# GLA's q and k in a stage of their own with seven products for eight, the gate's adaLN dots in quarters inside GLA, and a regrouped start

## The chip, the cores and the metric

The kernel runs on one core of a Trainium2 chip. The metric is the device time of one execution in microseconds. Every number comes from a profiled execution or from timed runs. The engines are called as in the profile: PE (TensorE), DVE (VectorE), ACT (ScalarE), POOL (GpSimd) and SP (SyncE); PEld is PE's loading of weights. SP and POOL also issue DMAs, each on a queue of its own.

## What is computed

A decoder layer with two parallel branches on x of 512 tokens by 2048 channels, all in float32. An adaLN modulation of x is projected; a gated linear attention (GLA, 4 heads, dk 256, dv 512) and a gated delta rule (GDN, 16 heads) run side by side; sigmoid gates merge them; an output projection, the adaLN gate, the residual and a layer norm follow.

```python
ada = jax.nn.silu(c) @ w_ada + b_ada
shift, scale, gate = jnp.split(ada, 3, axis=-1)
h = x * (1 + scale[:, None, :]) + shift[:, None, :]
u = h @ w_in
(gla_q, gla_k, gla_v, gla_g, gla_lr, gdn_q, gdn_k, gdn_v, gdn_z, gdn_b, gdn_a,
 merge_g) = jnp.split(u, _split_offsets(), axis=-1)
log_a = jax.nn.log_sigmoid((gla_lr @ w_gk2 + b_gk2).astype(f32)) / GLA_GATE_NORM
o_gla = _gla_chunked(_heads(gla_q...), _heads(gla_k...), _heads(gla_v...), _heads(log_a...))
y_gla = _gated_rmsnorm(o_gla, gla_norm_w, gla_g).astype(dt)
...
g_a, g_b = jnp.split(jax.nn.sigmoid(merge_g), 2, axis=-1)
merged = g_a * (y_gla @ w_branch[0]) + g_b * (y_gdn @ w_branch[1])
out = merged @ w_out
r = DEEPNORM_ALPHA * x + gate[:, None, :] * out
return _layernorm(r, ln_g, ln_b).astype(dt)
```

## The kernel before

**Products.** Each float32 operand is split into a high part and a low part, and a product is three matmuls, high by high, low by high and high by low (`mm3`, L99). The activation h lies in SBUF as 16 pairs `acth`, `actl` of 128 channels by 512 tokens. A unit of weights is 128x1024: SP loads it (512 KB, `wraw`), ACT rounds it to `whi` (L86), DVE subtracts to `wlo` (L88); `unit()` keeps three of them ahead. A column tile (`col_steps`, `proj_col`, L104 to L114) gives 128 output channels by 512 tokens: two units, 16 channel blocks, 48 matmuls of 512 columns. `proj_row` (L119) gives v in 192 such matmuls.

**The stages, in order of time.** Start: for each of the 16 blocks of h two dots on DVE (`ada_dot`, 128x2048 against silu of c, L215), two small operations into `scs`, then ACT makes `hf` (L247) and `acth` (L94) and DVE `actl` (L96). PE works on eight accumulators at a time and takes the blocks of h in three groups, (0,4), (4,9), (9,16), each for an "early" and a "first" set of columns; between groups the accumulators are drained into `part`, by ACT the first time (L279) and by DVE after (L281). GDN follows, with merge tiles woven in. (A merge tile is a column tile of the merge gates, put through tanh and stored to `d_mg`.) Then GLA, `gla_all`: per head q and k (four column tiles, L739 to L742), the decays `cum` (L743 to L755), the near diagonals (L767 to L799), v by `proj_row` (L801), levels 2 to 6 (L811 to L841, each with an `e` made of cum, k and q by DVE and ACT and sixteen small matmuls), the attention matrix `at` with its parts `atGt`, `atF`, `atqf` (L877 to L896), and four gate tiles (L907 to L915). Then a stage with the adaLN gate's 16 dots of 128x2048 (1 MB each through SP) beside seven merge tiles (L920 to L930). Last the branch products, the output projection and the layer norm; POOL's queue loads their inputs.

**What sets the order.** A scheduler writes each engine's instructions into one fixed row, from the program's text and its buffers; every engine takes its row in order, and an instruction that waits holds up all behind it. So where an instruction stands in the row matters as much as where it stands in the code.

## Time and profile before

| | us |
|---|---|
| median of 3 runs (lowest to highest) | 2410.5 (2410.38 to 2410.74) |
| the profiled execution | 2410.16 |
| its span, first to last instruction | 2408.4 |
| PE busy in the span | 2367.4 (98%) |
| DVE, ACT, POOL busy | 1510.7 (63%), 1054.5 (44%), 80.3 (3%) |
| granted TensorE clock, mean | 0.998 |

The profiled execution is 0.34 us below the median, and 1.8 us of it lie outside the span. A window row gives, for a stretch of the span, each engine's busy time with the number of its instructions. A row of the list of PE's waits says what PE stood for, in total, how often and at the longest. A timeline row is one instruction: its start, its length and, in square brackets, the idle time of the engine just before it with what ended it. The records of matmuls overlap, since they are pipelined: what one costs is read from the distance of starts, not from its length.

### The profile page before, as it was taken

The page shows a single profiled execution, that of the slowest core. Times are in us where ns is not written, and L with a number is a line of the kernel's source. Part 1 is how long each engine was busy: PE and PEld are TensorE (multiplying, and loading weights), DVE is VectorE, ACT ScalarE, POOL GpSimd, SP SyncE. Part 2 cuts the span into 40 slices and gives each one's busy share as a digit, 9 for nine tenths or more (in the row PEclk, how much of TensorE's full clock was granted, in tenths as well). Part 3 has the DMA queues.
Part 4 walks back from the last instruction along what each step waited for, and adds up shares of the span by engine and source line. Part 5 has one row for each costly group of instructions (what it writes and reads, how often), then busy time and mean ns, then how long its engine had stood idle before and what let it go on. Part 6 is the DMA issues. An engine that isn't in the chain of part 4 may idle for free.

```text
span 2408.4 us, 30754 instructions
## 1 busy us (share of the span) xinstructions
PE 2367.4 (98%) x11788; PEld 1943.4 (81%) x11788; DVE 1510.7 (63%) x2787; ACT 1054.5 (44%) x1647; POOL 80.3 (3%) x159
## 2 busy tenths in 40 slices
PE   6999999999999999999999999999999999999997
PEld 5888787888888888878888888888887888888886
DVE  7865677888777788873562745627475322344676
ACT  4335455555665555553442544425424311222353
POOL 0000000000000000000000000000002101010010
PEclk9999999999999999999999999999999999999999
DMA  9964333333333333233223222232298644445674
GB/s 393 369 216 136 114 100 100 100 100 102 100 100 103 108 104 96 96 96 119 94 75 110 88 91 88 76 114 88 92 350 284 214 140 138 146 147 184 215 246 148
DMA packets 119763, 347.92 MB, mean 144 GB/s; under 512 B 32448, under 2 KB 34880, under 8 KB 113472
## 3 DMA queue, kind: packets, MB, share of 16 engines
q1 hardware_dynamic: 109696, 313.45, 38.4%
q0 software_dynamic: 9920, 32.51, 3.9%
q8 instruction: 92, 1.51, 0.3%
q14 instruction: 55, 0.45, 0.1%
HBM read 318.57 MB, written 27.34 MB: 144 GB/s over the span
## 4 chain that ended last, share of the span: by engine, by line
PE 90%; DVE 4%; DMA 3%; issue 1%; ACT 1%; SPq 0%; POOL 0%; POOLq 0%; ACTq 0%; DVEq 0%
PE pj L100 22%; PE pj L101 21%; PE pj L102 21%; PE ms L158 2%; PE ms L157 2%; PE ms L159 2%; PE pj L133 2%; PE pj L134 2%; PE pj L135 2%; PE ms L100 1%; PE ms L102 1%; PE ms L101 1%; PE ms L840 1%; DVE junk L215 1%; DVE wlo L88 1%
## 5 line engine op out<-in xcount | busy, mean ns | idle before, releaser
L100 PE MATMUL pj<-acth,whi 128*128 128x512 f32 x2160 | 870.2, 403 | 20.8 <-ACT acth L94 19.2
L101 PE MATMUL pj<-acth,wlo 128*128 128x512 f32 x2160 | 845.2, 391 | 2.7 <-DVE wlo L88 2.7
L102 PE MATMUL pj<-actl,whi 128*128 128x512 f32 x2160 | 842.8, 391 | 0.0
L88 DVE TENSOR_TENSOR wlo<-wraw,whi 128x1024 fp32r<-128x1024 f32 x414 | 505.1, 1221 | 430.7 <-ACT whi L86 422.6
L86 ACT CAST whi<-wraw 128x1024 fp32r<-128x1024 f32 x414 | 433.7, 1048 | 585.4 <-PE pj L102 383.6
L100 PEld LDWEIGHTS pj<-acth,whi 128*128 128x128 f32 x2160 | 406.7, 188 | 101.4 <-ACT acth L94 20.0
L102 PEld LDWEIGHTS pj<-actl,whi 128*128 128x128 f32 x2160 | 405.9, 188 | 87.4 <-DVE actl L96 0.4
L101 PEld LDWEIGHTS pj<-acth,wlo 128*128 128x128 f32 x2160 | 407.0, 188 | 78.2 <-DVE wlo L88 4.1
L667 DVE TENSOR_TENSOR tmp<-vi,mi 128x8 f32<-128x8 f32 (+30 forms) x496 | 145.9, 294 | 13.3
L671 DVE TENSOR_REDUCE vi<-tmp 128x4 f32<-128x8 f32 (+30 forms) x496 | 111.1, 224 | 13.1
L215 DVE SCALAR_TENSOR_TENSOR junk<-wada,cs 128x2048 f32<-128x2048 f32 x48 | 109.7, 2285 | 4.7 <-DMA wada<-in_wada_dram 4.3
L100 PE MATMUL pj<-yh,whi 128*128 128x512 f32 x256 | 100.9, 394 | 0.0
L101 PE MATMUL pj<-yh,wlo 128*128 128x512 f32 x256 | 100.9, 394 | 0.0
L102 PE MATMUL pj<-yl,whi 128*128 128x512 f32 x256 | 100.9, 394 | 0.0
L158 PE MATMUL ms<-wlo,yh 128*128 128x512 f32 x240 | 94.8, 395 | 0.5 <-DVE wlo L88 0.5
L157 PE MATMUL ms<-whi,yh 128*128 128x512 f32 x240 | 93.8, 392 | 0.0
L159 PE MATMUL ms<-whi,yl 128*128 128x512 f32 x240 | 93.2, 388 | 0.0
L399 DVE SCALAR_TENSOR_TENSOR ac<-upad,convw,ac 128x512 f32<-128x512 f32 x96 | 71.5, 744 | 11.2 <-ACT ac L397 9.6
L133 PE MATMUL pj<-whi,acth 128*128 128x512 f32 x192 | 74.9, 390 | 0.0
L134 PE MATMUL pj<-wlo,acth 128*128 128x512 f32 x192 | 74.9, 390 | 0.0
L135 PE MATMUL pj<-whi,actl 128*128 128x512 f32 x192 | 74.7, 389 | 0.0
L100 PEld LDWEIGHTS pj<-yh,whi 128*128 128x128 f32 x256 | 47.9, 187 | 12.0
(304 smaller groups left out, 2768.8 us busy)
## 6 DMA issues: line engine op xcount, KB each, us to landing
wada<-in_wada_dram SPq DMA_DIRECT2D x48, 1024.0 KB, 8.7
wraw<-in_wqkv_dram SPq DMA_DIRECT2D x90, 512.0 KB, 3.4
wraw<-in_wbr_dram SPq DMA_DIRECT2D x64, 512.0 KB, 3.9
wraw<-in_wout_dram SPq DMA_DIRECT2D x64, 512.0 KB, 4.3
wraw<-in_wmg_dram SPq DMA_DIRECT2D x40, 512.0 KB, 3.6
wraw<-in_wz_dram SPq DMA_DIRECT2D x32, 512.0 KB, 3.5
wraw<-in_wlv_dram SPq DMA_DIRECT2D x32, 512.0 KB, 3.5
wraw<-in_wlg_dram SPq DMA_DIRECT2D x32, 512.0 KB, 3.4
```

Source lines behind the costliest of these rows:

```text
L86: S.copy(hi, raw)
L88: V.tensor_tensor(lo, raw, hi.bitcast(F32), ALU.subtract)
L100: PE.matmul(ps, wh, ah, start=start, stop=False)
L101: PE.matmul(ps, wl, ah, start=False, stop=False)
L102: PE.matmul(ps, wh, al, start=False, stop=stop)
L133: PE.matmul(pss[c], ah[:, a], hi[:, w], start=kt == 0, stop=False)
L134: PE.matmul(pss[c], ah[:, a], lo[:, w], start=False, stop=False)
L157: PE.matmul(pss[c], ah[:, a], hi, start=kt == 0, stop=False)
L158: PE.matmul(pss[c], ah[:, a], lo, start=False, stop=False)
L159: PE.matmul(pss[c], al[:, a], hi, start=False, stop=kt == KT - 1)
L215: V.scalar_tensor_tensor(junk, wt, 1.0, cs2, ALU.mult, ALU.mult, accum_out=acc_ss[:, j:j + 1])
L667: V.tensor_tensor(tmp[:, :, 0:n], vi[:, :, 0:n], mi[:, 0:n, i:i + 1].rearrange("p s o -> p o s").broadcast_to([P, 4, n]), ALU.mult)
```

## The change

1. **Start.** 13 matmuls on zeros run at the beginning. silu of c is made in four parts. The groups are four, (0,2), (2,5), (5,9), (9,16), so one drain of twice eight accumulators more. `acth` comes from xt in one ACT pass, and `hf` in a second one.
2. **q and k.** A new stage `qk_all` stands between GDN and GLA. Four merge tiles run in it first, during which h is rebuilt from x (16 reloads through POOL) and sums and differences of its four quarters are made, `sh`, `sl`. Then, for each of eight pairs of a q tile and a k tile, the four 128-column by 256-token by 1024-channel blocks of both are had from seven products in place of eight (the sums of a Strassen-Winograd scheme), each 24 matmuls of 256 columns. The weights are differences as well, made on DVE. q and k go to DRAM and come back per head (`load_qk`).
3. **GLA.** Two merge tiles stand at the beginning; the decays of the next head are made beside the gates of this one. The adaLN gate's dots are cut into quarters of 512 columns: 16 per head and one `cq`, written beside the four gate tiles, each loaded by POOL's queue (256 KB) into one of two buffers `wada`. The stage behind GLA is gone; five merge tiles stand ahead of the branch products where four stood.

```diff
-    G1, G2 = 4, 9
-    for lo, hi in ((0, G1), (G1, G2), (G2, KT)):
+    for lo, hi in ((0, 2), (2, 5), (5, 9), (9, KT)):
...
+        for _ in range(WARM):
+            PE.matmul(idle, zero[:, 0:P], zero, start=True, stop=True)
...
-            h.append(split_act(hf, actp, "act"))
+            lo = actp.tile([P, T], F32R, name="actl", tag="act", bufs=32)
+            V.tensor_tensor(lo, hf, hi.bitcast(F32), ALU.subtract)
...
-        made = [0, 1, 2, 3, 5, 6, 8, 9, 11, 12, 14, 15, 17, 18, 20, 21]
+        made = [0, 1, 2, 4, 5, 7, 8, 10, 11, 13, 15, 16, 18, 19, 21, 22]
...
+            def split_next():
+                p, x = todo.pop(0)
+                if x[0] == "t":
+                    a, b = {"t1": ("b12", "b11"), "t2": ("b22", "t1"), "t4": ("b21", "t2"),
+                            "t3": ("b22", "b12")}[x]
+                    src = wp.tile([P, 1024], F32, name="wraw", bufs=3)
+                    V.tensor_tensor(src, raws[p, a], raws[p, b], ALU.subtract)
...
+                product(x, quarter(0, 0), True, True)
+                S.copy(p1, x)
+                product(z, summed(0), True, True)
+                S.copy(z5, z)
+                product(y, summed(1), True, True)
+                V.tensor_tensor(u, y, p1, ALU.add)
+                product(v, quarter(1, 1), True, True)
+                product(x, quarter(0, 1), False, True)
+                S.activation(qo[:, 0:H], x, AF.Copy, scale=1.0 / 16.0)
+                product(z, summed(3), False, True)
...
+                product(y, summed(2), False, True)
...
+            def load_qk(hd):
                 q = lp.tile([P, 2, T], F32, name="q")
+                nc.gpsimd.dma_start(q, d_q[hd])
                 k = lp.tile([P, 2, T], F32, name="k")
+                nc.gpsimd.dma_start(k, d_k[hd])
...
-                for i in range(2):
-                    S.activation(q[:, i], proj_col(h), AF.Copy,
-                                 scale=1.0 / 16.0)
-                    S.copy(k[:, i], proj_col(h))
...
+                def gate_dot(j):
+                    wt = lp.tile([P, T], F32, name="wada", bufs=2)
+                    nc.gpsimd.dma_start(wt, io["wada"][32 + j][:, nq])
+                    V.scalar_tensor_tensor(wt, wt, 1.0, cq, ALU.mult, ALU.mult,
+                                           accum_out=acc_ss[:, 32 + 16 * hd + j:33 + 16 * hd + j])
...
-        for j in range(16):
-            ada_dot(adp, cs2, junk, 32 + j)
```

DVE's row in the start, near the first drains that DVE makes. Before, dots (L215), splits (L88) and `actl` (L96) alternate up to there:

```order
L88 TENSOR_TENSOR wlo<-wraw,whi 128x1024
L96 TENSOR_TENSOR actl<-hf,acth 128x512
L215 SCALAR_TENSOR_TENSOR junk,acc_ss<-wada,cs_93 128x2048
L281 TENSOR_TENSOR part<-pj,part 128x512
L242 TENSOR_SCALAR scs<-acc_ss,bada 128x1
L281 TENSOR_TENSOR part<-pj,part 128x512
```

After, at the first of the two sets that are drained by DVE and stood nowhere before:

```order
L92 TENSOR_TENSOR wlo<-wraw,whi 128x1024
L266 TENSOR_TENSOR actl<-hf,acth 128x512
L92 TENSOR_TENSOR wlo<-wraw,whi 128x1024
L300 TENSOR_TENSOR part<-pj,part 128x512 x3
L300 TENSOR_TENSOR part<-ot,part 128x512
L300 TENSOR_TENSOR part<-ms,part 128x512 x4
L223 SCALAR_TENSOR_TENSOR junk,acc_ss<-wada,cs_112 128x2048
L92 TENSOR_TENSOR wlo<-wraw,whi 128x1024
```

Eight drains stand in a block between the splits and the next dot; DVE's row now has 32 drains ahead of the last block of h where it had 16.

DVE's row in the v projection of GLA's second head. Before, up to the first level's e (L821):

```order
L88 TENSOR_TENSOR wlo<-wraw,whi 128x1024
L798 TENSOR_TENSOR at<-ms,ident 128x4x128
L88 TENSOR_TENSOR wlo<-wraw,whi 128x1024
L344 TENSOR_TENSOR sql<-e,sqh 128x512
L821 TENSOR_TENSOR e<-cum 128x128x4
```

After, the same stretch, where L1074 is a dot of the adaLN gate, L949 stands for L798 and L1069 makes `cq`:

```order
L92 TENSOR_TENSOR wlo<-wraw,whi 128x1024
L1074 SCALAR_TENSOR_TENSOR wada,acc_ss<-wada,cq 128x512 x4
L92 TENSOR_TENSOR wlo<-wraw,whi 128x1024
L1074 SCALAR_TENSOR_TENSOR wada,acc_ss<-wada,cq 128x512
L1091 TENSOR_TENSOR acc_ss<-acc_ss 128x16
L1069 SCALAR_TENSOR_TENSOR cq<-cq,wada 128x512
L949 TENSOR_TENSOR at<-ms,ident 128x4x128
L92 TENSOR_TENSOR wlo<-wraw,whi 128x1024
L363 TENSOR_TENSOR sql<-e,sqh 128x512
L1074 SCALAR_TENSOR_TENSOR wada,acc_ss<-wada,cq 128x512
```

Fifteen dots of the third head's quarter stand between this head's `wlo`, and eight of the fourth head's behind them, up to level 4; all 64 dots stand in the first two heads.

DVE's row behind level 6, where the attention matrix is put together. Before:

```order
L825 TENSOR_TENSOR e<-e,q 128x8x64
L883 TENSOR_TENSOR atGt<-at,atF 128x512
L883 TENSOR_TENSOR atGt<-at,atF 128x384
L883 TENSOR_TENSOR atqf<-at,atqf 128x256
L901 COPY total<-sq 128x512
```

After, in the second head:

```order
L976 TENSOR_TENSOR e<-e,q 128x8x64
L1074 SCALAR_TENSOR_TENSOR wada,acc_ss<-wada,cq 128x512 x2
L1034 TENSOR_TENSOR atGt<-at,atF 128x512
L937 TENSOR_TENSOR e<-k,q 128x1024
L1034 TENSOR_TENSOR atGt<-at,atF 128x384
L1034 TENSOR_TENSOR atqf<-at,atqf 128x256
```

The next head's first operation on the reloaded k and q, L937, has moved in between the two `atGt`.

## Rows read from the trace of the kernel before

**Rows 1.** The page's busy time, share of the span and count by engine.

```profile
PE 2367.4 (98%) x11788; PEld 1943.4 (81%) x11788; DVE 1510.7 (63%) x2787; ACT 1054.5 (44%) x1647; POOL 80.3 (3%) x159
```

**Rows 2.** PE's waits: what for, us in total, times, the longest.

```profile
PE pj L100 <- ACT acth L94: 19.2, 3, 16.7
PE pj L101 <- DVE wlo L88: 2.7, 4, 0.8
```

**Rows 3.** Windows (PE, PEld, DVE, ACT, POOL, PEclk, DMA, GB/s): a GLA head; the dots' stage.

```profile
1221.00:1372.50 151.50, 151.45 (x743) 126.34 (x742) 79.68 (x104) 62.69 (x82) 0.00 (x0) 1.00 0.27 91
...
1700.00:1860.00 160.00, 156.25 (x688) 127.67 (x687) 96.40 (x111) 56.31 (x74) 12.97 (x24) 1.00 0.72 254
```

**Rows 4.** Timeline of PE (start, length): the end of a v projection.

```profile
1367.11 0.40 PE L133 MATMUL pj<-whi,acth 128*128 128x512 f32 x1
...
1372.33 0.39 PE L135 MATMUL ot<-whi,actl 128*128 128x512 f32 x1
```

**Rows 5.** Timeline of PE and its weight loads: 256 columns, first head.

```profile
1243.46 0.28 PE L100 MATMUL ms<-atqf,v 128*128 128x256 f32 x1
1243.47 0.19 PEld L101 LDWEIGHTS ms<-atqf,vl 128*128 128x128 f32 x1
1243.58 0.28 PE L101 MATMUL ms<-atqf,vl 128*128 128x256 f32 x1
1243.59 0.19 PEld L102 LDWEIGHTS ms<-atqf,v 128*128 128x128 f32 x1
1243.70 0.28 PE L102 MATMUL ms<-atqf,v 128*128 128x256 f32 x1
```

**Rows 6.** Groups of DVE, 0 to 153 us: count, busy, mean ns, idle before.

```profile
L88 DVE TENSOR_TENSOR wlo<-wraw,whi 128x1024 fp32r<-128x1024 f32 x26 | 31.6, 1219 | 9.6 <-ACT whi L86 9.6
L96 DVE TENSOR_TENSOR actl<-hf,acth 128x512 fp32r<-128x512 f32 x16 | 11.0, 688 | 3.6 <-ACT acth L94 3.6
L281 DVE TENSOR_TENSOR part<-ms,part 128x512 f32<-128x512 f32 x8 | 5.0, 681 | 0.0
```

**Rows 7.** DMA issues of the page: count, KB each, median us to landing.

```profile
gt<-d_mg POOLq DMA_DIRECT2D x32, 256.0 KB, 3.2
...
yraw<-in_x_dram POOLq DMA_DIRECT2D x16, 256.0 KB, 4.2
```

**Rows 8.** Timeline of the start, ACT and PE.

```profile
14.43 0.81 ACT L247 ACTIVATE hf<-xt,scs 128x512 f32<-128x512 f32 x1
...
16.08 0.61 ACT L94 CAST acth<-hf 128x512 fp32r<-128x512 f32 x1
...
16.74 0.79 PE L100 MATMUL pj<-acth,whi 128*128 128x512 f32 x1 [16.74 <-ACT acth L94]
...
17.76 0.63 PE L100 MATMUL pj<-acth,whi 128*128 128x512 f32 x1
...
22.09 0.55 PE L100 MATMUL ms<-acth,whi 128*128 128x512 f32 x1
```

**Rows 9.** Timeline of DVE at the end of the start.

```profile
149.94 0.68 DVE L96 TENSOR_TENSOR actl<-hf,acth 128x512 fp32r<-128x512 f32 x1
...
154.90 0.69 DVE L281 TENSOR_TENSOR part<-pj,part 128x512 f32<-128x512 f32 x1 [3.14 <-PE pj L102]
```

**Rows 10.** Timeline of DVE and PE, second head's levels 4 to 6.

```profile
1374.32 1.22 DVE L88 TENSOR_TENSOR wlo<-wraw,whi 128x1024 fp32r<-128x1024 f32 x1 [0.93 <-ACT whi L86]
...
1380.60 2.02 PE L840 MATMUL ms<-e 128*128 128x128 f32 x16
...
1381.00 0.69 DVE L825 TENSOR_TENSOR e<-e,q 128x512 f32<-128x512 f32 x1
...
1388.29 0.68 DVE L825 TENSOR_TENSOR e<-e,q 128x512 f32<-128x512 f32 x1
...
1393.16 0.69 DVE L883 TENSOR_TENSOR atGt<-at,atF 128x512 fp32r<-128x512 f32 x1 [4.18 <-PE ms L873]
1394.07 0.56 DVE L883 TENSOR_TENSOR atGt<-at,atF 128x384 fp32r<-128x384 f32 x1 [0.22 <-ACT atF L882]
```

More of the change, by code (lines that the diff above doesn't have):

```diff
@@ L97, in split_act, with mm3 @@
         return hi, lo
-    def mm3(ps, wh, wl, ah, al, start, stop):
-        PE.matmul(ps, wh, ah, start=start, stop=False)
-        PE.matmul(ps, wl, ah, start=False, stop=False)
-        PE.matmul(ps, wh, al, start=False, stop=stop)
+    def mm3(ps, wh, wl, ah, al, start, stop, **kw):
+        PE.matmul(ps, wh, ah, start=start, stop=False, **kw)
+        PE.matmul(ps, wl, ah, start=False, stop=False, **kw)
+        PE.matmul(ps, wh, al, start=False, stop=stop, **kw)
     def col_steps(act):
@@ L184, in hybrid_layer @@
     use(io["wmg"], range(NMA, NMF))
+    NMS, NMG = NMF + 4, NMF + 6
+    use(io["wmg"], range(NMF, NMG))
     for hd in range(HL):
-        for i in range(2):
-            use(io["wlq"], [2 * hd + i])
-            use(io["wlk"], [2 * hd + i])
         use(io["wlv"], [hd], 8)
         use(io["wlg"], range(4 * hd, 4 * hd + 4))
-    use(io["wmg"], range(NMF, 20))
+    use(io["wmg"], range(NMG, 20))
     use(io["wbr"], range(2 * KT))
@@ L204, in silu_c @@
         cs2 = pool.tile([P, D], F32, name="cs2")
-        for n in (slice(0, D // 2), slice(D // 2, D)):
-            cb = pool.tile([P, D // 2], F32, name="wada", bufs=4)
-            nc.sync.dma_start(cb, io["c"][:, n].partition_broadcast(P))
-            S.activation(junk[:, n], cb, AF.Tanh, scale=0.5)
-            V.scalar_tensor_tensor(cs2[:, n], junk[:, n], 1.0, cb, ALU.add, ALU.mult)
+        for q in range(4):
+            n = slice(q * T, (q + 1) * T)
+            if q % 2 == 0:
+                cb = pool.tile([P, D // 2], F32, name="wada", bufs=4)
+                nc.sync.dma_start(cb, io["c"][:, q * T:(q + 2) * T].partition_broadcast(P))
+            cq = cb[:, q % 2 * T:(q % 2 + 1) * T]
+            S.activation(junk[:, n], cq, AF.Tanh, scale=0.5)
+            V.scalar_tensor_tensor(cs2[:, n], junk[:, n], 1.0, cq, ALU.add, ALU.mult)
         return cs2, junk
@@ L229, in hybrid_layer @@
     with tc.tile_pool(name="ada", bufs=1) as adp:
+        zero = adp.tile([P, T], F32, name="xt", bufs=2)
+        G.memset(zero, 0.0)
+        idle = psm.tile([P, T], F32, name="ms")
+        for _ in range(WARM):
+            PE.matmul(idle, zero[:, 0:P], zero, start=True, stop=True)
         cs2, junk = silu_c(adp)
         bada = cload("bada", [P, 48])
+        part = adp.tile([P, 16, T], F32, name="part")
         bada1 = cst.tile([P, 16], F32, name="bada1")
         V.tensor_scalar(bada1, bada[:, 16:32], 1.0, None, ALU.add)
-        scs = adp.tile([P, 32], F32, name="scs")
-        part = adp.tile([P, 16, T], F32, name="part")
         def make_h(kt):
@@ L755, in gla_all @@
                                          ALU.mult, ALU.add)
+                return cum
+            nxt = (*load_qk(0), decays(0))
+            for j in range(NMS, NMG):
+                merge_tile(12 + j)
+            for hd in range(HL):
+                q, k, cum = nxt
                 at = lp.tile([P, NC, T], F32, name="at")
@@ L915, in gla_all @@
                     nc.sync.dma_start(d_yl[4 * hd + j], of[:, j])
+            gcol = lp.tile([P, 16], F32, name="gcol", tag="cq")
+            for n in range(1, 4):
+                V.tensor_tensor(acc_ss[:, 32:48], acc_ss[:, 32:48],
+                                acc_ss[:, 32 + 16 * n:48 + 16 * n], ALU.add)
+            V.scalar_tensor_tensor(gcol, acc_ss[:, 32:48], 0.25, hbgate, ALU.mult, ALU.add)
+            nc.gpsimd.dma_start(d_gate.rearrange("j p -> p j"), gcol)
     gdn_all()
+    qk_all()
     gla_all()
-    NM = 12 + NMF
-    with tc.tile_pool(name="ada2", bufs=1) as adp:
-        cs2, junk = silu_c(adp)
-        gcol = adp.tile([P, 16], F32, name="gcol")
-        for j in range(16):
-            ada_dot(adp, cs2, junk, 32 + j)
-            V.tensor_scalar(gcol[:, j:j + 1], acc_ss[:, 32 + j:33 + j], 0.25,
-                            hbgate[:, j:j + 1], ALU.mult, ALU.add)
-            if j % 2 and j < 14:
-                merge_tile(NM)
-                NM += 1
-        nc.sync.dma_start(d_gate.rearrange("j p -> p j"), gcol)
     with tc.tile_pool(name="br", bufs=1) as bp:
@@ L941, in hybrid_layer @@
         done = 0
-        for j in range(NM, 2 * KT):
+        for j in range(12 + NMG, 2 * KT):
             for ps in col_steps(h):
                 done += 1
-                if done > 10 and done % 3 == 0 and len(yl) < KT:
+                if done > 20 and done % 3 == 0 and len(yl) < KT:
                     yl.append(yload(d_yl[len(yl)], bp, "y"))
```

128 lines of the change are left out of this document (119 added, 9 removed).

## The prediction

> **What bounds the kernel now.** I read the page's busy shares first: PE is busy for 2367.4 us of a 2408.4 us span, 98%; DVE has 63%, ACT 44% [rows 1]. So only two things can shorten this kernel: less time of TensorE's stream, or fewer of PE's idle 41 us. The list of PE's waits says where those are: 19.2 us on `acth`, three times, of which 16.7 us is the start; and 2.7 us on `wlo` [rows 2]. The windows put that last one in the stage after GLA (1700 to 1860, the gate's dots): 156.25 busy of 160, so 3.75 us idle [rows 3]. Inside GLA PE is busy for 151.45 of a head's 151.50 us, while DVE is busy for 79.68 [rows 3]. The change touches four places: the start, q and k of GLA, GLA's heads, and the stage after.
>
> **1. Seven products for eight.** Before: 16 tiles of 48 matmuls of 512 columns. Between 1367.11 and 1372.33 lie 23 of them, so one takes 5.22/23 = 0.227 us [rows 4]; 768 cost 174.3 us. After: 8 pairs x 7 products x 24 = 1344 matmuls of 256 columns, over 7/8 of the columns but 1.75 times the instructions and weight loads. The only 256-column products of the trace come in threes, each with weights of its own, 0.12 us apart (1243.46, 1243.58, 1243.70), their loads as far apart (1243.47, 1243.59) [rows 5]. 1344 x 0.12 = 161.3: **-13.0 us**. Half of the 512-column pitch, 0.1135, would give 152.5 (-21.8) and is the best end. Every weight load's record is 0.19 us long; if loads could not overlap, 1344 x 0.19 = 255 us, 81 more than now. The three loads that start 0.12 apart speak against that; but three in a row are not 1344, so 0.125 (168 us, -6.3) stays as the near bad end.
>
> Feeding: a pair's PE time is 168 x 0.12 = 20.2 us. DVE has in it 7 `wlo` and 4 weight differences of 1.22 us (the mean of `wlo<-wraw,whi`, 128x1024) and 5 drains, each at most the 0.68 of a 512-column drain [rows 6]: 16.8 us. It fits, at **0**. At the stage's entry the sums of h (16 reloads on POOL's queue, 16 ACT passes, 24 DVE operations: 16 of 512 columns, 8 of 1024, 20.8 us) lie under four merge tiles, 4 x 48 x 0.227 = 43.6 us of PE beside 8 `wlo`, 9.8 us. 30.6 fits into 43.6, but the POOL queue delivers its sixteen 256 KB at about 3.2 us each [rows 7] unless they overlap, and the last sum waits for the last of them: **+0.5**, from 0 to +3.
>
> **2. The start.** First level: the matmuls from 17.76 to 22.09 are 10 in 4.33 us, 0.433 each against 0.227 later, in a stretch that follows 16.74 us without a matmul [rows 8]. This is the lower of the clock's two levels, 1.2 against 2.4 GHz; thirteen such cost 13 x 0.206 = 2.7 us. The change's 13 matmuls on zeros run in that dead time, so -2.7 if the level then holds until the first real one. `acth` straight from xt takes the `hf` pass (14.43, 0.81) off the way to the first `acth` (16.08) [rows 8]: up to -1.6. More steps ahead of each new h take most of the 2.5 us of the two other `acth` waits (19.2 - 16.7). Up to -6.8 in all.
>
> But the stage ends on DVE. The last h needs its `actl`: issued at 149.94, over at 150.62, and one split later DVE stands 3.14 us until PE has finished its next accumulator at 154.90 [rows 9]. PE without a wait gets to the step that needs this h after 24 steps of 24 x 0.227 = 5.45, 130.8 us; from a first matmul at 15.1 that is 145.9. DVE meanwhile gets 16 more drains, since four groups of accumulators stand where three did: 16 x 0.62 [rows 6] = 9.9 us, all in front of that h, as the rows of the order show. From the end of cs2 (9.1 us) to 150.6 DVE has about 141.5 us, of which 9.6 wait for `whi` and 3.6 for `acth` [rows 6]. The rest of its idle time there is 2 us. With all those waits kept the h comes at 150.6 + 9.9 = 160.5; with none, at 147. Half kept gives 153, about where PE is today with its waits (16.74 + 130.8 + 2.7 + 2.5 = 152.7). So PE's gain of the first 40 us is handed back before the stage ends: **0**, from -6 to +7.
>
> **3. The dots in GLA.** Before, 16 dots of 128x2048 stood after GLA. Now 64 of 128x512 and four cq stand within GLA. In the code they sit one by one beside the gates, but the order puts all 64 into heads 0 and 1, and in head 1's v projection 23 lie between the wlo's, ahead of level 4's e. Work alone is no trouble: 64 x 0.69 = 44 us (the mean of a 512-column row of DVE's [rows 6]) where DVE idles 72 us a head [rows 3]. The trouble is that each dot waits in order for a load through POOL's queue with two buffers. A 256 KB load there took 3.2 us (`gt`), in the layer norm's stage 4.2 (`yraw` from x) [rows 7]. Buffer cycle: 3.2 + 0.7 for the dot + some 0.15 for semaphores, 4.05; two buffers: one dot per 2.0 us.
>
> Head 1, counted from the start of its v projection: that is 192 x 0.227 = 43.6 us, to 1372.56 [rows 4], and PE wants e 8.0 us later, at 1380.60, so at 51.6. Before, it got it with no slack: the matmuls start at 1380.60 on the first half while the last of e's operations starts at 1381.00 [rows 10]. Now 23 dots x 2.0 = 46 us, plus the work that stands between the last dot and e, 6.3 from `wlo` at 1374.32 to 1380.60 [rows 10]: 52.3, late by 0.7 if the loads never pause. They do pause whenever DVE has more than 2 us of other rows between dots with both buffers full: behind `at` (5 rows), between the two levels' dots (8 and 4 rows) and at `vl` such blocks lose, at 0.7 to 1.2 us a row, some 2, 4, 1.5 and 0.5 us, 8 in all, part of it made up by what is already loaded. So e is late by 0.7 to 8, or not at all where dots run ahead of PE before the projection; I take 4.5. Head 0 has two merge tiles in front but starts its loads only when GLA's buffers open; the same reckoning gives 0 to 8, taken at 5.5. PE has nothing to put there: its order is fixed. **+10**, from 0 to +16. Heads 2 and 3 have no dots: 0.
>
> The Trainium skill, "DMA: Bandwidth & Descriptors", section "Anatomy of one DMA — SWDGE (gpsimd) path", puts a transfer from the GpSimd queue at 2.0 us plus its bytes at 436 GB/s, 2.6 us for 256 KB. By that a dot would come every 1.75 us, the term would be about +5, and the sum 2402. The row says 3.2, so I stay with the row.
>
> **4. q and k through DRAM.** Each head reloads them, two loads of 512 KB on POOL's queue, into the buffers that level 6's e still reads; e was done at 1388.97 (1388.29 + 0.68), and between the two `atGt` (1393.16 and 1394.07 [rows 10]) DVE now has an operation on the new k and q. Two loads at the 3.2 to 4.2 us of half their size, plus issue, end between 1393 and 1396: the second `atGt` is late by 0 to 2. **+2.5** for three heads, from 0 to +6.
>
> **5. The stage after GLA** loses its dots and with them its 3.75 us of PE idling [rows 3]; the merge tiles move elsewhere and cost what they did. **-3.3**, from -2.7 to -3.75. The dots' 16 MB came at a DMA share of 0.72 [rows 3]; in GLA's two heads there is room.
>
> **Sum:** -13.0 + 0.5 + 0 + 10 + 2.5 - 3.3 = -3.3 us on the profiled execution's 2410.16: 2406.9. The median of the three runs is 2410.5, 0.34 above it: **2407.2 us**.
>
> **Rivals.**
> *The covers hold:* the dots slip into DVE's gaps (first end of 3 and 4: 0 and 0), the rest as above: 2407.2 - 12.5 = 2394.7. For it: DVE idles half of GLA, and before, its waits never reached PE. Against: zero slack at level 4.
> *The dots come slower still:* POOL's loads land in 4.2 us, as `yraw` did. A dot every 2.55 us: 23 x 0.55 = 12.6 more in head 1, half as much in head 0: 2407.2 + 19 = **2426**, slower than before. It decides from about 3.6 us of landing, where the gain of the products is gone. For it: the loads share the engines with 512 KB weight loads; against: `gt`'s 3.2 us were taken beside weight loads too. The Trainium skill, "SBUF — State Buffer", section "Who interferes with whom", says that DVE's two-port operations hold off what GpSimd writes for its transfers, not its two-input ones; the dots and splits are of the second kind, and no run here shows that stall.
> *The change does not do what it says at the products:* at 0.13 us a matmul they cost 174.7, no gain, and the rest leaves 2420; with loads that can't overlap, 2500.
> *DVE late at the start*, with all its waits kept: +7, 2414.
>
> **Chances.** Forecast (2403 to 2415): 0.42. Covers hold (2390 to 2402): 0.27. Dots slower (2415 to 2427): 0.23. Products without a gain (2420 and far above): 0.08. About 0.2%, 4.8 us, can be told from no change. Faster by more than that, under 2405.7: 0.27 and 0.15 of the forecast, 0.42. Slower, above 2415.3: 0.29. Within: 0.29. The forecast's own range is 2403 to 2415; with the covers' case down to 2391 and the slower dots up to 2424 some 8 in 10 is held.
>
> **What would show it.** Products: the 256-column rows of the qk stage 0.12 us apart, 20 us a pair, no wait for `wlo` in it. Start: first real matmul near 15.1 at the full level; a wait of PE for `acth` or `actl` behind step 24 if DVE ends it. Dots: rows of `wada` with a wait for a DMA in front, and PE waiting for `e` in heads 0 and 1, not in 2 and 3. Reload: DVE waiting for the DMA of k or q between the two `atGt`. The prediction is wrong if the loads of the dots land in under 2.5 us or over 4, or if the 256-column pitch isn't 0.12.

## The result and the profile after

The changed kernel takes 2424.2 us (median of 4 runs, 2422.7 to 2429.1), the kernel before on the same chip 2410.6 (2410.4 to 2415.3): a ratio of 1.0063, 95% interval 1.0051 to 1.0076. It is slower by some 14 us. Forecast were 2407.2 and, at the upper end, 2424. The profiled execution took 2423.1 us with a span of 2421.4, 13.0 longer than before, and a mean granted clock of 0.992 against 0.998.

The page's first line stands beside [rows 1]: DVE and POOL do more, PE's busy time is 4.4 us longer though its work shrank.

```profile
PE 2371.8 (98%) x12390; PEld 1967.8 (81%) x12390; DVE 1617.6 (67%) x3011; ACT 1099.3 (45%) x1713; POOL 140.0 (6%) x269
```

Windows over q and k's stage and over the first half of GLA (columns as in [rows 3]):

```profile
1172.00:1328.00 156.00, 156.00 (x1341) 155.84 (x1341) 118.99 (x126) 69.84 (x89) 7.58 (x14) 1.00 0.36 126
...
1350.00:1400.00 50.00, 44.92 (x191) 36.61 (x192) 39.53 (x70) 22.78 (x27) 6.99 (x13) 0.97 0.49 166
1400.00:1450.00 50.00, 44.16 (x259) 37.06 (x257) 37.16 (x74) 24.31 (x38) 10.21 (x19) 0.93 0.48 162
1450.00:1500.00 50.00, 47.44 (x209) 38.96 (x208) 38.99 (x66) 20.91 (x25) 5.91 (x11) 1.00 0.47 160
1500.00:1550.00 50.00, 42.79 (x222) 35.36 (x221) 38.07 (x73) 15.47 (x20) 9.68 (x18) 0.93 0.47 163
```

In q and k's stage PE never stops. In GLA, where before it was busy for 151.45 of 151.50 us [rows 3], it is idle for 3 to 7 of every 50 us, and the clock falls as well. The list of PE's waits from the end of q and k's stage to the first branch product (what for, us in total, times, longest) names the gaps:

```profile
PE ms L991 <- DVE e L976: 8.1, 2, 4.6
PE pj L140 <- DVE th L1083: 7.3, 3, 2.6
PE ms L370 <- DVE sql L363: 6.4, 3, 4.5
PE ms L369 <- ACT sqh L361: 2.7, 1, 2.7
PE ms L890 <- issue: 2.0, 1, 2.0
PE ms L109 <- DVE atGt L1034: 0.8, 2, 0.4
```

None of these stands in the list of before for the same part of the kernel, from GDN's end to the first branch product: there PE waits 2.7 us for `wlo` [rows 2] and 1.1 for `whi`, all of it in the dots' stage.

**Where the 13.0 us come from.** I cut both timelines of PE at the same places: end of GDN, end of q and k, first branch product, end of the span. Waits are the bracketed idle times; the rest is the time at which PE's matmuls followed one another.

| stretch | before | after | difference |
|---|---|---|---|
| to the end of GDN | 1123.4 | 1120.3 | -3.0 |
| q and k's products | 174.3 | 156.2 | -18.1 |
| GLA and merge tiles, PE's waits | 3.75 | 27.2 | +23.5 |
| GLA and merge tiles, matmuls themselves | 562.5 | 573.6 | +11.1 |
| branches to the end | 544.5 | 544.0 | -0.5 |

The matmuls of the fourth row are the same in number and shape in both kernels. Their 11.1 us more are the lower clock behind the waits: from q and k's stage to the first branch product, 548 us, the granted clock is 0.98, where the same stages of before have 1.00, and 2% of 548 us are 11 us. Of the -3.0 of the first row the start has 0.3: PE begins its 25th step, which needs the last block of h, at 153.68 us, before at 154.02. The rest is no effect to count on: in the runs below with this start, q and k begin anywhere from 1172.1 to 1178.7 us.

**The dots' waits.** Timeline of DVE and PE of the changed kernel, first head (start, length; in brackets the idle time before and what ended it). L1074 is a dot, L949 and L363 belong to the near diagonals, L976 to level 4's e:

```profile
1387.36 0.69 DVE L1074 SCALAR_TENSOR_TENSOR wada<-wada,cq 128x512 f32<-128x512 f32 x1 [2.37 <-DMA wada<-in_wada_dram]
...
1389.62 0.69 DVE L1074 SCALAR_TENSOR_TENSOR wada<-wada,cq 128x512 f32<-128x512 f32 x1 [1.55 <-DMA wada<-in_wada_dram]
...
1390.24 0.68 DVE L949 TENSOR_TENSOR at<-ms,ident 128x512 f32<-128x512 f32 x1
1390.84 0.68 DVE L363 TENSOR_TENSOR sql<-e,sqh 128x512 fp32r<-128x512 f32 x1
...
1391.58 0.80 PE L370 MATMUL ms<-sql,onesr 128*128 128x512 f32 x1 [4.49 <-DVE sql L363]
...
1409.82 0.69 DVE L1074 SCALAR_TENSOR_TENSOR wada<-wada,cq 128x512 f32<-128x512 f32 x1 [2.10 <-DMA wada<-in_wada_dram]
...
1416.51 0.68 DVE L976 TENSOR_TENSOR e<-e,q 128x512 f32<-128x512 f32 x1
...
1417.34 3.76 PE L991 MATMUL ms<-e 128*128 128x128 f32 x16 [4.62 <-DVE e L976]
```

DVE stands 2.37 and 1.55 us for loads, 3.92 together; `sql`, next but one in its row, is late, and PE stands 4.49 us. The same follows at e, 4.62 us. The last row shows the clock too: these sixteen matmuls took 3.76 us, the same sixteen of before 2.02 [rows 10].

The second head loses 3.45 us at e (1541.34) in the same way, behind a dot that waited 1.75 us at 1533.82. Its near diagonals are late too, 2.65 and 1.10 us (1514.89 and 1516.50), but over ACT's row. There L1068, which makes the next `cq`, stands ahead of a `whi` and of `sqh`, and waits for c, which POOL's queue loads into one of the dots' two buffers:

```profile
1512.76 0.63 ACT L1068 ACTIVATE cq<-wada 128x512 f32<-128x512 f32 x1 [10.81 <-DMA wada<-in_c_dram]
```

**A wait of another kind.** Timeline of ACT, DVE and PE where the second head's v projection begins (L1082 and L1083 drain the last gate tile, L140 is the projection):

```profile
1478.28 0.59 ACT L1082 ACTIVATE th<-pj 128x512 f32<-128x512 f32 x1
...
1479.87 0.67 DVE L1083 SCALAR_TENSOR_TENSOR th<-th,pj 128x512 f32<-128x512 f32 x1
...
1480.60 0.50 PE L140 MATMUL pj<-whi,acth 128*128 128x512 f32 x1 [2.56 <-DVE th L1083]
```

The projection holds four accumulators at once, one of which is still being read by the last gate tile's drain. Before, the next head's four q and k tiles stood between the two, 43.5 us of PE, and hid it. The seven-product stage took them away. Each of the heads two to four pays: 2.56, 2.56, 2.23.

The 2.0 us at L890, the first product of the decays, for which the list names no releaser, are of this kind too. That product reads `lrT`, the small input of GLA's decay gate. ACT waits for its load, DVE makes its low part, and PE starts 0.1 us after that, here and in every other run with the seven-product stage, where this wait is 2.0 to 6.4 us long:

```profile
1349.04 0.62 ACT L848 CAST lrT<-of 80x512 fp32r<-80x512 f32 x1 [2.54 <-DMA of<-d_lr]
1349.81 0.68 DVE L849 TENSOR_TENSOR lrT<-of,lrT 16x512 fp32r<-16x512 f32 x1
...
1350.59 0.70 PE L890 MATMUL ms<-lrT,wgk 80*128 80x512 f32 x2 [2.02 <-issue]
```

Before, `lrT` was ready 23 us ahead of that product, under the first head's q and k tiles:

```profile
1151.57 0.68 DVE L707 TENSOR_TENSOR lrT<-of,lrT 16x512 fp32r<-16x512 f32 x1 [0.45 <-ACT lrT L706]
...
1175.77 0.62 PE L746 MATMUL ms<-lrT,wgk 80*128 80x512 f32 x2
```

### The profile page after: what moved, and what is told of

Same layout as the page of the kernel before. It is cut to its first block, busy times and chain, and to the rows that moved or that the text cites. A ratio compares the mean times of both kernels' runs of the same rounds, so it can differ in the third digit from the quotient of the medians.

```text
span 2421.4 us, 32551 instructions
## 1 busy us (share of the span) xinstructions
PE 2371.8 (98%) x12390; PEld 1967.8 (81%) x12390; DVE 1617.6 (67%) x3011; ACT 1099.3 (45%) x1713; POOL 140.0 (6%) x269
## 4 chain that ended last, share of the span: by engine, by line
PE 76%; issue 11%; DVE 7%; DMA 3%; ACT 2%; POOL 1%; SPq 0%; POOLq 0%; DVEq 0%; ACTq 0%
PE pj L107 18%; PE pj L109 18%; PE pj L108 18%; PE ms L109 2%; PE ms L107 2%; PE ms L165 2%; PE ms L108 2%; PE ms L164 2%; PE ms L166 2%; DVE wlo L92 1%; DVE junk L223 1%; POOL wada L1073 1%; PE ms L569 1%; PE ms L612 1%; PE ms L579 1%
## 5 line engine op out<-in xcount | busy, mean ns | idle before, releaser
L107 PE MATMUL pj<-acth,whi 128*128 128x512 f32 (+1 forms) x1968 | 786.2, 401 | 4.0 <-ACT acth L262 3.4
L108 PE MATMUL pj<-acth,wlo 128*128 128x512 f32 (+1 forms) x1968 | 761.0, 387 | 0.9 <-DVE wlo L92 0.9
L109 PE MATMUL pj<-actl,whi 128*128 128x512 f32 (+1 forms) x1968 | 760.1, 387 | 0.5 <-DVE actl L266 0.5
L92 DVE TENSOR_TENSOR wlo<-wraw,whi 128x1024 fp32r<-128x1024 f32 x382 | 465.7, 1222 | 315.7 <-ACT whi L90 311.7
L90 ACT CAST whi<-wraw 128x1024 fp32r<-128x1024 f32 x382 | 399.2, 1047 | 525.2 <-PE pj L109 316.9
L109 PEld LDWEIGHTS pj<-actl,whi 128*128 128x128 f32 x1968 | 369.8, 188 | 78.4 <-DVE actl L266 1.1
L107 PEld LDWEIGHTS pj<-acth,whi 128*128 128x128 f32 x1968 | 370.5, 188 | 73.3 <-ACT acth L262 4.7
L108 PEld LDWEIGHTS pj<-acth,wlo 128*128 128x128 f32 x1968 | 370.9, 188 | 65.8 <-DVE wlo L92 1.5
L140 PE MATMUL pj<-whi,acth 128*128 128x512 f32 x192 | 77.1, 402 | 7.3 <-DVE th L1083 7.3
L109 PE MATMUL ms<-actl,whi 128*128 128x512 f32 (+1 forms) x224 | 76.9, 343 | 0.0
L108 PE MATMUL ms<-acth,wlo 128*128 128x512 f32 (+1 forms) x224 | 76.9, 343 | 0.0
```

The lines of the kernel that those rows point to most:

```text
L90: S.copy(hi, raw)
L92: V.tensor_tensor(lo, raw, hi.bitcast(F32), ALU.subtract)
L107: PE.matmul(ps, wh, ah, start=start, stop=False, **kw)
L108: PE.matmul(ps, wl, ah, start=False, stop=False, **kw)
L109: PE.matmul(ps, wh, al, start=False, stop=stop, **kw)
L140: PE.matmul(pss[c], ah[:, a], hi[:, w], start=kt == 0, stop=False)
```

## The experiments

Theory A: the dots' loads hold DVE's fixed row and so PE (sql, sqh, e: 17.1 us of waits, of which 0.8, at the norm of the first head's output, follow no dot). Theory B: the missing q and k tiles uncover the gate's drain (th: 7.3). Rival C: the traffic of the dots, or DVE's added 44 us, costs time wherever it is. All ratios are to the kernel before on the same chip, with a 95% interval.

**1. No dots.**

```diff
-                    for n, pg in enumerate(col_steps(h)):
-                        if n % 4 == 1:
-                            gate_dot(4 * j + n // 4)
+                    pg = proj_col(h)
```

> The changed kernel without the adaLN gate's dots in GLA and their loads; the gate is its bias part alone. Theory 1 (the loss sits in DVE's row: dots that wait in order for their loads hold up sql and e, and PE's clock falls after each such wait): PE's waits for sql, sqh and e in heads 0 and 1, 17 us in the changed kernel's trace, go, and with them some 8 us at the lower clock level; 2424 - 25 = about 2399. The three waits of 2.2 to 2.6 us for th at the start of a v projection stay. Rival (DVE is late there for other reasons, the hoisted decays and near diagonals): the waits for sql and e stay and the time is above 2415.

Measured: 2413.1 us, ratio 0.9997 (0.9987 to 1.0006). The stretch from q and k to the branches fell from 548.6 to 532.1 us. So the dots cost some 16 us in all, not the whole loss, and the 2399 expected were missed. The waits for sql, sqh and e are gone; those for th are not, and grew. PE's waits in that stretch:

```profile
PE pj L140 <- DVE th L1068: 8.2, 3, 3.8
PE ms L890 <- issue: 5.0, 1, 5.0
PE ms L109 <- DVE atGt L1034: 2.9, 3, 1.4
```

**2. The dots beside the first branch's products**, four a tile, six buffers shared with the y loads.

```diff
+            for n, ps in enumerate(col_steps(yl)):
+                if n % 4 == 1:
+                    gate_dot(j // 4, 4 * (j % 4) + n // 4)
```

> The changed kernel with the 64 dots moved out of GLA to the first branch's products, where DVE is busy for some 14 of 50 us, with six load buffers in place of two. Nothing is left out. Theory 1: as without dots, about 2399, since 64 x 0.69 = 44 us fit under the 87 us of eight column tiles there. Rival (the dots cost wherever they stand, because their 16 MB through POOL's queue delay the branch's own loads): above 2410.

Measured: 2435.2 us, 1.0092 (1.0075 to 1.0109). GLA gained as in the first experiment (533.2 us), but the stretch from the branches on went from 544.0 to 565.7. PE waits there for `wlo` and `whi`, 12.0 us in eight waits of over 0.9 us. For the larger part dots stand in DVE's row ahead of the splits and wait for loads, whose landing is now 5.0 us. In three of the waits, 4.6 us, ACT had stood for a load of the second branch's y, which shares its buffers and POOL's queue with the dots, and `whi` stood behind it. ACT's waits for y:

```profile
ACT acth L101 <- DMA yraw<-d_yg: 55.9, 12, 7.8
```

A free DVE is no better place if a dot still waits in the row.

**3. A cover: one merge tile ahead of each v projection** of heads two to four, dots left in GLA. (The loads of y for the first branch then begin earlier, with the first of the two merge tiles that stay behind GLA.)

```diff
+                if hd:
+                    merge_tile(12 + NMG + hd - 1)
```

> The changed kernel with one of the five late merge tiles ahead of the v projection of each of heads 1, 2 and 3, so that the accumulator of the last gate tile has time to be read. Theory 2 (the removed q and k tiles used to cover the way from the last gate tile over tanh and th to the next free accumulator): the three waits of 2.56, 2.56 and 2.23 us go, 7.4 us, and some 3 us of lower clock behind two of them; 2424 - 10 = about 2414. Rival (heads 0 and 1 are bound by DVE's row, the extra tile only moves the wait to e): only the waits of heads 2 and 3 go, 2418 or more.

Measured: 2436.9 us, 1.0098 (1.0083 to 1.0113). The th waits are gone, which B wants, but the scheduler laid the rows anew. The near diagonals wait longer, and the second `atGt` of the second head stands behind the next head's first operation on its reloaded q (L941). In POOL's queue that reload came behind the store of the gate, which left 13.33 us late. PE's waits, then the rows of POOL and DVE:

```profile
PE ms L372 <- DVE sql L365: 14.9, 3, 8.8
PE ms L109 <- DVE atGt L1038: 12.4, 2, 12.1
PE ms L995 <- DVE e L980: 6.7, 2, 4.1
```

```profile
1567.74 1.19 POOL L1098 DMA_DIRECT2D d_gate<-gcol  x1 [13.33 <-DVE wlo L92]
...
1586.50 1.23 DVE L941 TENSOR_TENSOR e<-k,q 128x1024 f32<-128x1024 f32 x1 [12.31 <-DMA q<-d_q]
```

**4. Both, 2 and 3.**

> The two edits together: dots at the first branch's products, a merge tile ahead of the v projections of heads 1 to 3. Theories 1 and 2 together: 2424 - 25 - 10 = about 2389, below the kernel before by 21, which is the 18 of the seven products, the 3.75 of the stage that is gone and a little of the start less the remaining waits. Rival (the gain of the products is eaten by something else in GLA): between 2400 and 2410.

Measured: 2420.0 us, 1.0024 (1.0015 to 1.0034). GLA is clean now, 514.1 us for 548.6: with the dots and the drain both dealt with, 34.5 of the 34.6 us are back. So A and B together explain GLA. The loss sits in the branches, where PE waits 12.7 us for `wlo` and 4.6 for `whi`, behind waiting dots and, in four waits of 7.2 us together, behind loads of y that ACT waits for.

**5 and 6. Dots beside each head's own gates**, where the code has them: buffers shared with `th`, three in all; the second with the cover.

```diff
-                    wt = lp.tile([P, T], F32, name="wada", bufs=2)
+                    wt = lp.tile([P, T], F32, name="wada", tag="th", bufs=3)
```

> The changed kernel with one edit: the dots' load buffers and th of the gate tiles take turns in the same three buffers, so that the scheduler can't place a dot more than about three ahead of its gate tile; the 64 dots then stand in DVE's row beside the gate tiles of all four heads, 16 each. Theory 1a (not the dots cost, but the place in DVE's row to which they were drawn): PE's waits for sql, sqh and e go and the stretch from the last product of the qk stage to the first branch product falls by the 16.5 us that it fell without any dots, so the time is about 14 to 16 us under the changed kernel, 2 us under the kernel before. The three waits for th stay. Rival 1b (64 loads through POOL's queue and 44 us of DVE cost the same anywhere in GLA): no more than 5 us under the changed kernel.

> The same, and a merge tile ahead of the v projections of heads 1 to 3. With the dots held at their gate tiles the extra tile can't draw them elsewhere, as it did in the run with the tile alone, so theory 2 can show: the three waits for th go (8.3 us) and the lower clock behind them, 3 to 8 us; 20 to 24 us under the kernel before by ratio, 0.991. Rival: with q and k gone, DVE's row is late for something else in GLA, and the waits only change their name; ratio above 0.997.

Measured: 2434.4 us, 1.0100 (1.0085 to 1.0115), and with the cover 2418.8, 1.0035 (1.0022 to 1.0048). The waits for sql and e are gone in both, so these came from the order. But th made PE wait 8.3, 8.1 and 7.4 us: its drain stands in DVE's row behind near-diagonal operations of the next head and a dot that waits for its load (1.73 us at 1470.64, less in the later heads). The cover took that, and waits for `wlo` and `mth` came instead. My theory that only the place in the head mattered fell: the gates have drains and splits of their own that then stand behind the dots.

**7. A third buffer for the dots in GLA**, one less for the squares.

```diff
-                    wt = lp.tile([P, T], F32, name="wada", bufs=2)
+                    wt = lp.tile([P, T], F32, name="wada", bufs=3)
```

> The changed kernel with three load buffers for the dots where it has two (and one for sq where it has two, to make room). By the prediction's reckoning a dot then comes every 1.35 us instead of every 2.0 and the waits for sql and e fall to near nothing: 10 to 16 us under the changed kernel. Theory 1a: the scheduler plans with loads faster than they are, so with a third buffer it draws the dots still further ahead; the waits stay, within 8 us of the changed kernel.

Measured: 2422.4 us, 1.0047 (1.0031 to 1.0063): some 4 us better than the change, at the edge of what can be told, where 10 to 16 were expected. DVE waits 21.8 us for dots' loads for 29.7, PE still 6.9 for th, 4.1 for e, 2.9 for sql, and 6.4 for `lrT`, ahead of whose low part a waiting dot stands.

**8. The start and the products by themselves.** On a version with the cover and two dots a tile over both branches: that version (x16), without the cover (x19), with eight products (x17), with the start of before (x18).

> Dots at two a column tile over both branches (32 tiles), load buffers shared with gt in three, and the merge tile ahead of the v projections of heads 1 to 3. Theory 3: GLA has lost the 43.5 us of q and k tiles per head that covered the head's decays, near diagonals and last gate, and a dot that waits in order for a load through POOL's queue costs wherever DVE's row has no slack for it; with a merge tile as cover and one dot in 5.4 us, both are gone. The stretch from the last qk product to the first branch product then takes 514 us (as with both edits), the rest to the end 545 us (as without dots) where it took 571 and 569: ratio to before 0.991, about 2389. Rival (the 16 MB through POOL's queue hold up the branch's own loads and so wlo however thin they are spread): the rest takes 560 or more, ratio above 0.997.

> The same without the three merge tiles in GLA: they stand with the late ones again. Theory 3: the waits for th come back, 8 us, and with them the lower clock: the kernel is 14 to 20 us slower than the one with the tiles. Rival (the tiles had moved the dots, nothing else): within 5 us of it.

> The kernel with spread dots and cover, but q and k in the same stage by eight products, that is 16 column tiles of 48 matmuls of 512 columns, stored and reloaded alike; the sums of h are left out, since nothing needs them. All theories: the products alone are worth the difference of 174.3 and the 156.0 us that the 1344 matmuls took (0.116 each), so 18 us slower than the kernel with seven. Rival (the seven products give some of it back by their DVE work or at the stage's entry): 10 us or less.

> The kernel with spread dots and cover, but the start as it was: no matmuls on zeros, three groups, acth by way of hf. The prediction put the new start at 0 (from -6 to +7), as DVE's sixteen extra drains hand back what PE gains in the first 40 us; so within 3 us of the kernel with the new start. Rival (the start is worth its warm clock and waits): 5 to 7 us slower.

| | us | ratio | interval |
|---|---|---|---|
| x16, base | 2424.0 | 1.0067 | 1.0050 to 1.0084 |
| x19, no cover | 2433.2 | 1.0102 | 1.0085 to 1.0118 |
| x17, eight products | 2434.8 | 1.0106 | 1.0091 to 1.0121 |
| x18, old start | 2424.5 | 1.0065 | 1.0042 to 1.0087 |

What the start is worth can't be told from nothing, as forecast: 0.5 us in time, where the intervals leave some 7 us either way, and 0.2 us at PE's 25th step (153.56 for 153.72). The seven products are worth 10.8 us in the whole kernel, with some 5.5 either way, and 14.4 by the place where the branches begin, less than the 18.1 of their stage. The cover is worth 9.2 us in time and 16.7 in GLA, where th's three waits, 8.3 us, come back without it; as in the ledger, waits cost more than their length. The base missed its expectation: spreading the dots thinner did not help, as each still waits in the row. Its timelines of DVE and PE:

```profile
1939.65 0.69 DVE L1121 SCALAR_TENSOR_TENSOR wada<-wada,cq 128x512 f32<-128x512 f32 x1 [6.17 <-DMA wada<-in_wada_dram]
...
1940.27 1.22 DVE L92 TENSOR_TENSOR wlo<-wraw,whi 128x1024 fp32r<-128x1024 f32 x1
...
1941.54 0.50 PE L108 MATMUL pj<-yh,wlo 128*128 128x512 f32 x1 [2.14 <-DVE wlo L92]
```

A further paced version, four dots a tile in buffers shared with `gt`, gave 2415.4 us, 1.002 (1.001 to 1.003), with DVE waiting 78 us for dots' loads.

> As the run with both edits, the dots beside the first branch's products, but their buffers now take turns with gt, so that they are spread over the sixteen column tiles at four each where the scheduler had drawn them into the first eight. Theory 1a: the 13.6 us of waits for wlo and the 4.6 for whi in the branch stage go with the lower clock behind them, 27 us in all between first branch product and end; ratio to before 0.991. Rival 1b: the 16 MB through POOL's queue hold up wlo there whatever their spacing; ratio above 1.

**9. Pinning.** Four dots a tile in the first branch, each reading as its factor a one that ACT makes from the accumulator of the tile before: a dot cannot be laid before that tile's end, by when its load should have landed.

```diff
+            S.activation(t[:, 0:1], ps[:, 0:1], AF.Identity, scale=0.0, bias=1.0)
...
-            V.scalar_tensor_tensor(wt, wt, 1.0, cqs[hd], ALU.mult, ALU.mult,
+            V.scalar_tensor_tensor(wt, wt, pins[-1][:, 0:1], cqs[hd], ALU.mult, ALU.mult,
```

> Dots beside the first branch's products, four a column tile, with the merge tile ahead of the v projections of heads 1 to 3; every dot now also reads a one that ACT makes from the accumulator of the column tile before, so it can't stand in DVE's row ahead of that tile's end, while its load is free to start a tile earlier (six buffers). Theory 4 (a dot costs by standing in DVE's row and waiting there for a load that is slower than the scheduler takes it to be; DVE's time and the traffic cost nothing): DVE's waits for these loads, 20 to 78 us in the earlier runs, fall under 10, PE's waits for wlo in the branch stage under 4, from first branch product to end 545 to 550 us; ratio to before 0.991 to 0.993. Rival (the traffic of 16 MB through POOL's queue is what holds up wlo): 560 us or more for that stretch, ratio above 0.997.

Measured: 2427.2 us, 1.0068 (1.0053 to 1.0083). The dots' waits are gone, 0.4 us in the branches. But the loads of the second branch's y stand behind the dots' loads in POOL's queue, and these wait for a buffer of the ring that both share, one that the split of an earlier y (`actl`) gives back. A load of y takes 7.6 us to land, where the changed kernel has 4.2. First row ACT's longest wait between 1844 and 2130 us, second POOL's:

```profile
ACT acth L101 <- DMA yraw<-d_yg: 158.1, 16, 13.4
...
POOL wada L1129 <- DVE actl L103: 105.9, 14, 9.8
```

The wait had moved from DVE's row to ACT's, behind POOL's queue.

**10. No dots, with the cover.**

> The changed kernel without the adaLN gate's dots (the gate is its bias part alone) and with the merge tile ahead of the v projections of heads 1 to 3: what is left when both suspected causes are gone. Theories 1 and 3: stretch from the last qk product to the first branch product 514 us, from there to the end 545: ratio to before 0.990 to 0.992. Rival (a third cause in GLA): over 525 us in the first stretch.

Measured: 2399.4 us, 0.9945 (0.9925 to 0.9964). Without dots there was then a gain of 10 us. It is no floor: from q and k to the branches it took 522.0 us, where 514 were expected and the fourth experiment had 514.1, with 5.8 us of waits for `lrT` and 3.6 for `atGt`; and the twelfth experiment, with all its dots, is faster.

**11 and 12. Pinned dots with a ring of three buffers of their own** (shared only with loads that come before or after them), three dots a tile over both branches; then the same with the first dot four tiles later.

```diff
-            wt = bp.tile([P, T], F32, name="wada", tag="yraw", bufs=6)
+            wt = bp.tile([P, T], F32, name="wada", tag="wt", bufs=3)
...
-                i = 3 * j + n // 5
+                i = 3 * (j - 4) + n // 5
```

> As z7_pinned, but the dots' loads no longer share a ring of buffers with the loads of y: three buffers of their own (shared only with x, which comes after the dots), two for y; three dots a column tile over 22 column tiles. In z7_pinned DVE's waits for the dots' loads were gone (0.4 us) but ACT stood 158 us for y's loads, which waited in POOL's queue for a buffer that a pinned dot gave back, and whi stood behind them. Theory 4 (a load that DVE or ACT waits for in its fixed row costs, the traffic doesn't): ACT's waits for y fall under 20 us, PE's waits for wlo and whi in the branch stage under 5, stretch from first branch product to end 547 to 552 us (without dots 547.8), ratio to before 0.992 to 0.996. Rival (the traffic through POOL's queue): 560 us or more.

> As z8_rings, but the dots begin four column tiles later, when y's loads are over. In z8_rings PE's only waits left in the branch stage, 6.3 us, and most of ACT's 37.5 us for y stood in those four tiles. Theory 4: both go, the stretch from first branch product to end falls from 557 to about 549 us (without dots 547.8), ratio to before 0.992 to 0.995. Rival (traffic): it stays at 555 or more, the ratio at 0.996 or more.

Measured: 2405.1 us, 0.9962 (0.9948 to 0.9976), with 6.3 us of waits for splits in the first four tiles; then **2393.0 us (2390.6 to 2393.5), 0.9913 (0.9900 to 0.9927)**, faster than both kernels. Windows of the last one, and of x16 (experiment 8), over the same 200 us of the branches:

```profile
1850.00:2050.00 200.00, 200.00 (x862) 160.93 (x861) 100.57 (x167) 54.98 (x99) 54.46 (x102) 1.00 0.69 229
```

```profile
1850.00:2050.00 200.00, 180.80 (x755) 140.06 (x754) 82.91 (x138) 47.17 (x56) 47.77 (x89) 1.00 0.60 200
```

The winner moves more bytes there (229 against 200 GB/s), DVE does more work, and PE does not stop once. All that it waits for between q and k's stage and the branches:

```profile
PE ms L892 <- issue: 2.1, 1, 2.1
PE ms L109 <- DVE atGt L1038: 1.7, 3, 0.8
```

DVE still stood for loads of dots there, five times, without PE stopping:

```profile
DVE wada L1131 <- DMA wada<-in_wada_dram: 9.2, 5, 5.7
```

From the first branch product to the end this kernel takes 545.0 us with the 64 dots, the changed kernel 544.0 without them. So C falls: the dots and their 16 MB cost some 1 us at most where a dot's wait doesn't reach PE.

**13. The changed kernel again**, on the chip of the last run.

> The changed kernel itself once more, on the same chip as the kernel with the later dots: ratio to before 1.005 to 1.0075 as when it was first timed. If it were below 1.002, the loss would be one of the first chip alone.

Measured: 2429.4 us, 1.0064 (1.0050 to 1.0077), with the same waits: 4.92 for sql, 3.94 and 5.19 for e, 2.58, 2.61 and 2.23 for th.

## Why the prediction was wrong

**Products: right, under-sized.** Forecast -13.0 at 0.12 us a matmul, with -21.8 as the best end; the stage gave -18.1: 1344 matmuls in 156.2 us, 0.116 each. The timeline's rows are alternately 0.11 and 0.12 apart:

```profile
1172.73 0.28 PE L107 MATMUL ms<-acth,whi 128*128 128x256 f32 x1
1172.84 0.28 PE L108 MATMUL ms<-acth,wlo 128*128 128x256 f32 x1
1172.96 0.28 PE L109 MATMUL ms<-actl,whi 128*128 128x256 f32 x1
```

Loads overlapped and DVE kept up (119 of 156 us), so the pitch read from three in a row [rows 5] held for 1344, and the entry's +0.5 did not come. The rival "no gain from the products" fell.

**Start: right in size, its mechanism not shown.** Forecast 0 with DVE as the late one. The timeline of PE shows the gain of its first 20 us, and where it went:

```profile
15.19 0.97 PE L107 MATMUL pj<-acth,whi 128*128 128x512 f32 x3 [0.51 <-ACT acth L262]
...
23.86 0.50 PE L107 MATMUL pj<-acth,whi 128*128 128x512 f32 x1 [2.91 <-ACT acth L262]
```

The first product comes at 15.19 (forecast 15.1), and the first twelve are 0.24 us apart (15.19 to 18.07) where before it was 0.433 [rows 8]; but the second group's h is 2.91 us late. The last `actl` was issued at 154.05, against 153 reckoned. But the sign that I gave for DVE ending the stage, a wait of PE for `acth` or `actl` behind step 24, is not there: PE begins its 25th step at 153.68 (before 154.02). It lost its gain on the way, in the 2.91 us above with slower matmuls behind them (0.43 us apart from 25.97 to 28.53) and in two waits for DVE, 0.85 for `wlo` at 72.68 and 0.59 for a drain at 100.62. With the start of before, x18 differs from x16 by 0.5 us.

**Reload of q and k: right in place, over-sized.** Forecast +2.5. The second `atGt` is late by 0.42 and 0.33 us, +0.8. Each load took longer than I took (4.7 and 5.8 us for 512 KB in the list of DMA issues), but was issued early enough.

**The stage after GLA: right**, -3.75 for -3.3.

**The dots in GLA: the step that failed, +10 forecast and +37.5 measured** (27.2 of waits less atGt's 0.8, and 11.1 of clock). The step's +10, all of it at e, was the prediction's only price for new waits in GLA besides the reload's. Much of its input was right: the median load landed in 3.3 us where I took 3.2, all 64 dots ran in the first two heads (1343 to 1563 us), PE waited for e in just these. Three things were missing:

1. *The near diagonals have as little slack as e.* I followed only e, "with no slack" [rows 10], and gave each head one delay of 4.5 to 5.5. In the trace each head has two, at the near diagonals' squares and at e; the two heads lost 16.3 us of waits where I had 10. One of the four came over ACT's row and the load for `cq`, which had no price in my sum.
2. *What q and k's tiles had covered.* I costed them as 174.3 us of products and never asked what lay under them. "Heads 2 and 3 have no dots: 0" is false by the same mistake. Three th waits, 7.3 us; and 2.0 for `lrT` at the decays' first product (5.0 in the first experiment).
3. *What a wait does to the clock.* I counted waits at their length. The granted clock fell behind most of them, 11.1 us more.

Together 10 + 6.3 + 7.3 + 2.0 + 11.1 = 36.7; the 0.8 us at the norm of the first head's output stay unexplained. The rival "the dots come slower still" gave 2426, close to the measured time, but by landings of 4.2 us and by waits at e alone. The median of the 64 landings is 3.3 us, the mean 3.7, and 17 took 4.0 or more, among them the one behind the wait at 1391.58 (issued at 1385.29, landed at 1389.53). So slow loads have a share in the 6.3 us, how large no run shows; with th, `lrT` and the clock, 20 us, they have nothing to do. In the main it is a right number by a wrong mechanism. And the conditions that I gave for being wrong (landing under 2.5 or over 4, a pitch other than 0.12) were not what happened: 3.3, and 0.116. None asked for lost cover. Two details of the sum were off as well. By its own figures the forecast gain of 3.3 us is gone from 3.4 us of landing, not 3.6; and the 0.15 us for semaphores in its buffer cycle stands in no row, while the trace of the changed kernel has 0.3 us from a dot's end to the next issue alone (1384.99 to 1385.29).

The Trainium skill, "DMA: Bandwidth & Descriptors", section "Anatomy of one DMA — SWDGE (gpsimd) path", by whose fit a 256 KB load takes an estimated 2.6 us, does not agree with this trace, which has 3.3 as the median of 64:

```profile
wada<-in_wada_dram POOLq DMA_DIRECT2D x64, 256.0 KB, 3.3
```

## What to carry to other kernels

When work of TensorE is taken out or moved, list what ran beneath it on the other engines, above all the drain of the accumulator that the next long product wants, and small inputs that are made there; that is part of the price of the change. An operation that needs a transfer and stands in the same in-order row as a feeder of the bottleneck can hold that feeder up wherever it is put, so tie it to something that ends after its transfer has landed and give that transfer buffers and a queue place that nobody else waits for. Then the work itself is nearly free: the same 64 dots cost 16 us in the changed kernel and some 1 us at most in the last one.

## What the runs showed of the hardware

The price of a wait on TensorE was not its length. Windows of 5 us of the changed kernel, behind the waits of 4.49 at 1391.58, 4.62 at 1417.34 and 2.56 at 1480.60 and around the 2.56 at 1602.46:

```profile
1415.00:1420.00 5.00, 2.66 (x12) 2.69 (x13) 4.65 (x10) 1.93 (x2) 0.59 (x2) 0.50 0.12 46
1420.00:1425.00 5.00, 5.00 (x48) 4.02 (x47) 3.25 (x6) 2.03 (x4) 1.02 (x2) 0.82 0.30 105
1390.00:1395.00 5.00, 3.42 (x9) 2.78 (x10) 5.00 (x10) 1.05 (x2) 0.77 (x2) 0.66 0.46 160
...
1600.00:1605.00 5.00, 2.54 (x6) 1.99 (x7) 4.29 (x8) 1.30 (x2) 0.00 (x0) 0.77 0.45 159
1480.00:1485.00 5.00, 4.41 (x19) 3.66 (x20) 3.65 (x7) 0.38 (x1) 1.77 (x4) 1.00 0.69 229
```

The granted clock (the third number from the right; 0.50 is the lower of its two levels) fell behind three of these four waits, but not behind the one at 1480.60, though that at 1602.46 was just as long, 2.56 us. So waits of at most 4.6 us, 27 us in all, brought 11 us of slower matmuls with them here, and a wait's length alone doesn't tell whether it will. A sequence of 256-column products, each with new weights, ran at 0.116 us a matmul for 156 us on end, within 3% of half the 512-column pitch of 0.227 [rows 4].
